# The tile of the masked scores as a fifth room, by turns, for the gates that multiply the pooled products

## The chip, the core and the metric

The kernel runs on one core of one Trainium2 chip. The core has a matrix engine (TensorE, PE in the profile, with its weight loads listed as PEld), a vector engine (VectorE, DVE), a scalar engine (ScalarE, ACT), a general engine (GpSimd, POOL), and SyncE (SP), whose queue issues nearly all DMA transfers. Each engine works through its own list of instructions in order and waits at an instruction until what it needs is there. On-chip tiles lie in SBUF; matrix products are accumulated in banks of PSUM.

The metric is the device time in microseconds (us) of one execution. Lower is better.

## The reference, cut to what matters

One decoder block on a sequence of 1024 tokens with 1024 channels, in float32. The projection of the input is split into parts for a gated recurrence (branch a), a pooling mixer (branch b) and two gates. The change touches only how branch b meets its gate:

```
proj = x @ w_in          # -> q, f, i, o_gate, pool_v, gate_a, gate_b
a = HGRN2(q, f, i) ... @ w_a
pooled[g] = causal mean over (2, 4, 8, 16)[g] tokens of pool_v[g] - pool_v[g]
b = concat_g(pooled[g] @ w_pool[g]) * pool_scale
merged = sigmoid(gate_a) * a + sigmoid(gate_b) * b
x = LN(alpha * x + merged @ w_out)
x = LN(alpha * x + relu(x @ w_up)**2 @ w_down)
```

## The kernel before, in words

Activations are kept transposed: 128 channels on the partitions, tokens along the free dimension, in two halves `u` of 512 tokens. Channels come in 8 blocks `j` of 128. Every float32 product is made of three matmuls on a high and a low part of each operand. ScalarE makes the high part (a CAST) and VectorE the low part (a subtraction). The large projections use a seven-product scheme (helper `pair`, lines 219, 221 and 222 for its matmuls), and the recurrence over 16 half-heads is woven between these products. For TensorE the order of instructions is the order of the code in this stage; for the other engines and the DMA queues the planner sets it from its own costs and the dependencies.

When the recurrence is over, the products of the pooling branch are woven in the same way between the products of the gates 6 and 7 (`pool_products`, called through `beside` with the counts of `POOL_AFTER`). There are 16 of them, and this text numbers them 1 to 16 in the order in which they run. Group `g` (0 to 3) and token half `u` give two each, one for each channel block `j = 2g + i`. So product 5 is block 2 with half 0, product 10 is block 5 with half 0; products 13 and 15 are those of block 7, which go another way (line 903) and are of no concern here. For each of the other 14:

- a room `t` of 128 x 512 is taken (line 896) and the gate `sigmoid(gate_b)`, which was put into DRAM earlier as `gbd[j][u]`, is loaded into it by SP (line 898: "load n" below);
- TensorE makes the product with six matmuls into a PSUM bank of the tag `tr`, of which there are two (lines 114 to 116, by `mm3` in line 900), so that product n + 2 needs the bank of product n;
- VectorE reads the bank, multiplies by the scale and by the gate in the room, and writes the result into the room (line 905: "multiplication n");
- SP stores the room to DRAM as `pbd[j][u]` (line 906: "store n").

In the kernel before, all these rooms come from the tag `f`, a ring of 4 that was used by the recurrence earlier (`RINGS`, `f=4`). So load n + 4 goes into the room of product n and waits until store n has landed. As SP issues in order, whatever stands behind a waiting load in its list waits too.

The tile `att` (128 x 4 x 128, that is 512 numbers on each partition) holds the masked scores of the recurrence. VectorE writes it for every half-head with a copy under the mask (line 1116), and TensorE reads it as the weights of the products with the values (line 1153). It was set to zero once, and the places outside of the mask have to stay zero as long as the recurrence runs. It is not used after the last half-head.

Of the kernel before, what the change touches and what calls it, by code (L numbers as in the profile page):

```python
# [52 lines left out]
def tile_hybrid_block(  # L53
# [36 lines left out]
    def nm(s):  # L90
        seq[0] += 1
        return f"{s}_{seq[0]}"
# [7 lines left out]
    def ps_tile(tag="pj", bufs=4):  # L100
        if tag == "hg":
            hg_tags.append(hg_tags.pop(0))
            tag, bufs = hg_tags[-1], 1
        return pp.tile([P, HALF], F32, tag=tag, name=nm("ps_" + tag), bufs=bufs)

    def f(t):
        return t.bitcast(F32)


    def mm3(ps, terms):  # L110

        n = len(terms)
        for i, (wh, wl, xh, xl) in enumerate(terms):
            PE.matmul(ps, wh, xh, start=i == 0, stop=False)  # L114
            PE.matmul(ps, wh, xl, start=False, stop=False)  # L115
            PE.matmul(ps, wl, xh, start=False, stop=i == n - 1)  # L116
# [8 lines left out]
    def split(src, tile_of):  # L125
        hi, lo = tile_of(), tile_of()
        A.copy(hi, src)
        V.tensor_sub(lo, src, f(hi))
        return hi, lo
# [130 lines left out]
    @contextmanager  # L260
    def behind_weight(n=-1):

        with tc.issue_after(hi_of[n]), tc.issue_after(lo_of[n]):
            yield
# [195 lines left out]
    def row_tile():  # L460
        return w_tile().rearrange("p k c -> p (k c)")
# [259 lines left out]
    def loaded(src, tile_of):  # L721
        t = tile_of()
        nc.sync.dma_start(out=t, in_=src)
        return t
# [31 lines left out]
    with tc.tile_pool(name="tmp", bufs=1, side="right", reuse_waits="tile") as tmp:  # L756
# [3 lines left out]
        att = hgp.tile([P, CH, P], F32, name="att")  # L760
# [11 lines left out]
        def tt(tag, dtype=F32):  # L772
            pool = tmp if tag in ("q", "f", "og", "v") else hgp
            return pool.tile([P, HALF], dtype, tag=tag, name=nm(tag), bufs=RINGS.get(tag, 1))
# [77 lines left out]
        def pool_products():  # L852

            def ring(*tags):
                tags = list(tags)
                def tile(dtype=F32):
                    tags.append(tags.pop(0))
                    return tt(tags[-1], dtype)
                return tile

            pod_tile, w_tiles = ring("tA", "tA", "st", "st", "tH", "tH"), ring("tD", "tE", "tF", "og")

            def wide(t):
                return t.rearrange("p (k c) -> p k c", c=2 * P)

            def load(g, u):
                raw = None
                if not u:
                    raw = loaded(w_pool[g].rearrange("(k p) c -> p k c", p=P), lambda: wide(tt("tC")))
                return raw, [loaded(pod[2 * g + i][u], pod_tile) for i in range(2)]  # L870

            def parts(g, u, raw, pods):
                with behind_weight():
                    if raw is not None:
                        w_parts[g] = split(raw, lambda: wide(w_tiles(F32R)))
                    made = []
                    for t in pods:
                        hi, lo = row_tile(), row_tile()
                        pool_parts[:] = A.copy(hi, t).ins, V.tensor_sub(lo, t, f(hi)).ins
                        made.append((hi, lo))  # L880
                    return made

            w_parts = {}
            todo = [(g, u) for g in range(CH) for u in range(2)]
            soon = [load(*todo[0]), load(*todo[1])]
            pl = parts(*todo[0], *soon.pop(0))
            yield
            for n, (g, u) in enumerate(todo):
                if n + 2 < len(todo):
                    soon.append(load(*todo[n + 2]))  # L890
                wh, wl = w_parts[g]
                for i in (0, 1) if g < CH - 1 else (1, 0):
                    w = slice(i * P, (i + 1) * P)
                    j = 2 * g + i
                    final = j == KT - 1
                    t = tt("v") if final else tt("f")
                    if not final:
                        nc.sync.dma_start(out=t, in_=gbd[j][u])
                    ps = ps_tile("tr", 2)
                    mm3(ps, [(wh[:, c, w], wl[:, c, w], *pl[c]) for c in range(2)])  # L900
                    if final:
                        held[u] = t
                        A.activation(t, ps, AF.Copy, scale=pscale[:, j : j + 1])
                    else:
                        V.scalar_tensor_tensor(t, ps, pscale[:, j : j + 1], t, ALU.mult, ALU.mult)
                        nc.sync.dma_start(out=pbd[j][u], in_=t)
                    if i == (1 if g < CH - 1 else 0) and soon:
                        pl = parts(*todo[n + 1], *soon.pop(0))
                    yield
# [312 lines left out]
        with tc.manual_schedule(engines={mybir.EngineType.PE}):  # L1222
            turns = turning[0] = recurrence()
            output_gates(0)
            for what, j in ORDER:
                if what == "inputs":
                    head_inputs(j)
                else:
                    dict(gates=gates, pooled=pooled, output_gates=output_gates)[what](j)
            finish_pending()  # L1230
            stream = pool_products()
            next(stream)
            for j, counts in POOL_AFTER.items():
                turning[0] = beside(stream, counts)
                gates(j)
                finish_pending()
            for _ in turns:
                pass
            turning[0] = iter(())
# [373 lines left out]
    for b in range(NBLK):  # L1613
# [3 lines left out]
        if last:  # L1617

            for ring in (dh, dw):
                t = fw.tile([P, M, 2, HALF], F32R, tag="draw", name=nm("dx"), bufs=2)  # L1620
                ring[:0] = [(t[:, n], t[:, n + 1]) for n in (0, 2)]
        for i, (name, slot, chain, fresh, (u, nh)) in enumerate(steps):
# [13 lines left out]
            for c in range(CH):  # L1636
                t = u * CH + c
# [49 lines left out]
```

## Time and profile before

| | us |
|---|---|
| median of 3 runs | 1437.62 (1436.34 to 1438.64) |
| profiled execution, its own time | 1434.66 |
| profiled execution, span from first to last instruction | 1433.0 |
| TensorE busy in that span | 1420.8 |
| VectorE, ScalarE, GpSimd busy | 1099.2, 753.2, 110.9 |
| mean granted TensorE clock | 0.999 |

The profile gives busy time by engine, then by line of the code, and for idle time what ended it. A row such as `PE ps_tr L114 <- DVE f L905: 1.4, 1, 1.4` reads: TensorE, before an instruction of line 114 that writes a tile `ps_tr`, waited for a VectorE instruction of line 905 that wrote a tile `f`, 1.4 us in total, once, longest 1.4. In a timeline each row gives start, duration, engine, line, operation, output and inputs, and in brackets the idle time just before and what ended it. Numbers of buffers are left out of the names.

### The profile page before, as it was taken

The numbers are of one execution on the slowest core, as the hardware profiler recorded it, in microseconds if no ns is written. First come the engines' busy times: TensorE is split into PE (matmuls) and PEld (weight loads), VectorE is DVE, ScalarE is ACT, GpSimd is POOL, SyncE is SP. The second block draws the span as 40 slices with busy tenths as digits, with TensorE's granted clock in tenths as the row PEclk, the third lists the DMA queues.
The fourth block names the chain that finished last, engine by engine and source line by source line (L and its number), as shares of the span: only waits on it lengthen the run. The fifth ranks groups of instructions, "written<-read, shape, count | busy, mean of one in ns | idle before, by whom it ended". The sixth has DMA issues, their size and how long they took to land.

```text
span 1433.0 us, 21208 instructions
## 1 busy us (share of the span) xinstructions
PE 1420.8 (99%) x7499; PEld 1180.1 (82%) x7499; DVE 1099.2 (77%) x1832; ACT 753.2 (53%) x1376; POOL 110.9 (8%) x300
## 2 busy tenths in 40 slices
PE   9999999999999999999999999999999999999997
PEld 7888888888888888878888888888888888888886
DVE  6967887897797796679965697666666887777978
ACT  5445566566656656455522376555556433433534
POOL 0002011111212110100003000000000100000000
PEclk9999999999999999999999999999999999999999
DMA  7142254444444546899551315444457864444422
GB/s 272 60 140 89 90 131 148 126 115 150 113 118 133 150 123 190 237 322 340 182 198 74 103 59 188 153 159 161 162 177 243 299 235 146 150 151 157 132 74 118
DMA packets 187179, 228.18 MB, mean 159 GB/s; under 512 B 12576, under 2 KB 111168, under 8 KB 187072
## 3 DMA queue, kind: packets, MB, share of 16 engines
q1 hardware_dynamic: 180464, 210.94, 44.6%
q0 software_dynamic: 5824, 13.63, 4.7%
q10 hardware_dynamic: 784, 2.25, 0.5%
q8 instruction: 59, 0.97, 0.3%
q14 instruction: 48, 0.39, 0.1%
HBM read 149.70 MB, written 77.07 MB: 158 GB/s over the span
## 4 chain that ended last, share of the span: by engine, by line
PE 95%; DVE 2%; DMA 1%; ACT 1%; issue 1%; POOL 0%; DVEq 0%; ACTq 0%; SPq 0%; POOLq 0%
PE ps_pj L219 16%; PE ps_pj L222 16%; PE ps_pj L221 16%; PE ps_pj L1565 4%; PE ps_pj L1566 4%; PE ps_pj L1564 4%; PE ps_pj L115 2%; PE ps_pj L114 2%; PE ps_pj L116 2%; PE ps_tr L1566 2%; PE ps_tr L1565 2%; PE ps_tr L1564 2%; PE ps_hg L219 1%; PE ps_sc L219 1%; PE ps_sc L222 1%; PE ps_hg L221 1%
## 5 line engine op out<-in xcount | busy, mean ns | idle before, releaser
L219 PE MATMUL ps_pj<-act,w 128*128 128x512 f32 x1068 | 419.9, 393 | 0.3 <-ACT c L303 0.2
L222 PE MATMUL ps_pj<-act,w 128*128 128x512 f32 x1068 | 415.3, 390 | 0.0
L221 PE MATMUL ps_pj<-act,w 128*128 128x512 f32 x1068 | 415.3, 389 | 0.0
L256 ACT CAST w<-raw 128x512 fp32r<-128x512 f32 x303 | 187.7, 621 | 255.4 <-PE ps_pj L221 169.7
L257 DVE TENSOR_TENSOR w<-raw,w 128x512 fp32r<-128x512 f32 x303 | 207.2, 686 | 93.6 <-ACT w L256 92.3
L219 PEld LDWEIGHTS ps_pj<-act,w 128*128 128x128 f32 x1068 | 200.5, 188 | 44.1 <-ACT c L303 1.3
L222 PEld LDWEIGHTS ps_pj<-act,w 128*128 128x128 f32 x1068 | 200.5, 188 | 42.4
L221 PEld LDWEIGHTS ps_pj<-act,w 128*128 128x128 f32 x1068 | 200.6, 188 | 40.5
L1526 ACT CAST act<-act 128x1024 fp32r<-128x1024 f32 x66 | 67.0, 1050 | 108.2 <-issue 35.0
L1527 DVE TENSOR_TENSOR act<-act,act 128x1024 fp32r<-128x1024 f32 x66 | 79.4, 1220 | 18.1 <-ACT act L1526 18.1
L1566 PE MATMUL ps_pj<-act,act 128*128 128x512 f32 x240 | 93.0, 389 | 0.0
L1565 PE MATMUL ps_pj<-act,act 128*128 128x512 f32 x240 | 93.0, 389 | 0.0
L1564 PE MATMUL ps_pj<-act,act 128*128 128x512 f32 x240 | 92.5, 389 | 0.0
L307 DVE TENSOR_TENSOR c<-c,ps_pj 128x512 f32<-128x512 f32 x91 | 62.1, 682 | 32.5 <-PE ps_pj L222 31.8
L303 ACT COPY c<-ps_pj 128x512 f32<-128x512 f32 x92 | 53.3, 581 | 3.0 <-PE ps_pj L222 1.9
L1564 PEld LDWEIGHTS ps_pj<-act,act 128*128 128x128 f32 x240 | 45.0, 188 | 9.4
L1565 PEld LDWEIGHTS ps_pj<-act,act 128*128 128x128 f32 x240 | 45.0, 188 | 9.4
L1566 PEld LDWEIGHTS ps_pj<-act,act 128*128 128x128 f32 x240 | 45.0, 188 | 9.3
L312 DVE TENSOR_TENSOR raw<-raw,raw 128x512 f32<-128x512 f32 x43 | 29.6, 689 | 25.5 <-DMA raw<-in_w_in_dram 16.1
L1435 ACT ACTIVATE c<-c 128x512 f32<-128x512 f32 x61 | 38.5, 632 | 1.7
L1434 ACT ACTIVATE c<-c 128x512 f32<-128x512 f32 x46 | 29.0, 632 | 16.4 <-DVE c L307 16.4
L751 POOL DMA_DIRECT2D s<-og x28 | 24.9, 1161 | 133.2 <-DVE og L1177 133.2
(433 smaller groups left out, 2684.6 us busy)
## 6 DMA issues: line engine op xcount, KB each, us to landing
h<-c SPq DMA_DIRECT2D x106, 256.0 KB, 3.0
raw<-in_w_in_dram SPq DMA_DIRECT2D x100, 256.0 KB, 3.3
act<-h SPq DMA_DIRECT2D x78, 256.0 KB, 3.0
draw<-in_w_down_dram SPq DMA_DIRECT2D x16, 1024.0 KB, 8.2
raw<-in_w_up_dram SPq DMA_DIRECT2D x56, 256.0 KB, 2.9
hf<-h SPq DMA_DIRECT2D x34, 256.0 KB, 3.0
s<-og POOLq DMA_DIRECT2D x28, 256.0 KB, 6.4
v<-v SPq DMA_DIRECT2D x16, 256.0 KB, 3.5
```

Source lines behind the costliest of these rows:

```text
L219: PE.matmul(ps, wh[:, k], th, start=first and k == 0, stop=False, skip_group_check=True)
L221: PE.matmul(ps, wh[:, k], tl, start=False, stop=False, skip_group_check=True)
L222: PE.matmul(ps, wl[:, k], th, start=False, stop=k == CH - 1, skip_group_check=True)
L256: hi_of.append(A.copy(hi, src).ins)
L257: lo_of.append(V.tensor_sub(lo, src, f(hi)).ins)
L303: noted(A.copy(t, ps))
L307: last_add[0] = V.tensor_add(t, t, ps).ins
L1526: A.copy(hi, src)
L1527: V.tensor_sub(lo, src, f(hi))
L1564: PE.matmul(ps, hh[:, w], wh, start=fresh and n == 0, stop=False, skip_group_check=True)
L1565: PE.matmul(ps, hh[:, w], wl, start=False, stop=False, skip_group_check=True)
L1566: PE.matmul(ps, hl[:, w], wh, start=False, stop=n == M - 1, skip_group_check=True)
```

## The change

Every fifth room is no longer taken from the ring `f`. It is the tile `att`, seen as 128 x 512. The counter `rooms_used` counts all 16 products, those of block 7 included, so `att` is the room of products 5 and 10 (product 15 is of block 7 and takes its own tile as before).

```diff
-            w_parts = {}
+            w_parts, rooms_used = {}, [0]
...
                     final = j == KT - 1
-                    t = tt("v") if final else tt("f")
+                    rooms_used[0] += 1
+                    t = tt("v") if final else tt("f") if rooms_used[0] % 5 else att.rearrange("p c q -> p (c q)")
                     if not final:
                         nc.sync.dma_start(out=t, in_=gbd[j][u])
```

The lines below it move down by one (line 898 becomes 899, 905 becomes 906, 906 becomes 907). The two kernels have the same instructions in the same order on TensorE, VectorE, ScalarE and GpSimd, but for two multiplications of line 906 that now work on `att`. Only SP's list differs, between the loads for the first pooled products and the end of the 14 loads.

The first place is SP's list just behind the recurrence. `po` is a stored pooled input and `st`, `tA`, `tH` are the tiles that it is loaded into, `raw` a block of weights, `ga` a store of a gate. The last number of a name is the number of the buffer. Before:

```order
L723 DMA st_6613<-po_1_993 128x512
L723 DMA tA_6611<-po_0_994 128x512
L723 DMA st_6615<-po_1_995 128x512
L723 DMA tH_6683<-po_0_996 128x512
L230 DMA raw_6923<-in_w_in_dram 128x4x128
```

And now:

```order
L723 DMA st_6613<-po_1_993 128x512
L899 DMA att<-gb_0_980 128x512
L723 DMA tA_6611<-po_0_994 128x512
L723 DMA st_6615<-po_1_995 128x512
L723 DMA tH_6683<-po_0_996 128x512
L230 DMA raw_6922<-in_w_in_dram 128x4x128
```

Load 5 (`gb_0_980` is `gbd[2][0]`) has moved up to here. It stood 18 rows further down, behind store 1.

The second place is SP's list in the middle of the pooled products, from store 5 on (`pb_0_1012`). Stores are named `pb`, loads of the gates are those out of `gb`: `gb_1_983` is the gate of product 8, `gb_0_984` of 9, `gb_0_986` of 10, `gb_1_985` of 11, `gb_1_987` of 12. `gb_0_988<-c` is a store of another gate. Before:

```order
L906 DMA pb_0_1012<-f_6840 128x512
L898 DMA f_6900<-gb_1_983 128x512
L723 DMA st_7011<-po_1_1005 128x512
L906 DMA pb_0_1014<-f_6851 128x512
L723 DMA st_7013<-po_1_1007 128x512
L898 DMA f_6961<-gb_0_984 128x512
L842 DMA gb_0_988<-c_6882 128x512
L230 DMA raw_7200<-in_w_a_dram 128x4x128
L906 DMA pb_1_1013<-f_6889 128x512
L898 DMA f_6972<-gb_0_986 128x512
L906 DMA pb_1_1015<-f_6900 128x512
L898 DMA f_7015<-gb_1_985 128x512
```

And now:

```order
L907 DMA pb_0_1012<-att 128x512
L899 DMA f_6960<-gb_0_984 128x512
L723 DMA st_7009<-po_1_1005 128x512
L907 DMA pb_0_1014<-f_6850 128x512
L723 DMA st_7011<-po_1_1007 128x512
L899 DMA att<-gb_0_986 128x512
L842 DMA gb_0_988<-c_6881 128x512
L230 DMA raw_7198<-in_w_a_dram 128x4x128
L907 DMA pb_1_1013<-f_6888 128x512
L899 DMA f_7013<-gb_1_985 128x512
L907 DMA pb_1_1015<-f_6899 128x512
L899 DMA f_7024<-gb_1_987 128x512
```

The stores and the loads of other things stand as they stood. In each place in which a gate was loaded, the gate of the next product is loaded now: load 9 where load 8 was, load 10, into `att`, where load 9 was, and in the same way load 8 where load 7 was, some rows ahead of this piece. Load 9 waits for store 4, as load 8 did; the second load into `att` waits for store 5, which is the store out of `att`.


## The prediction

> **What bounds the kernel now.** I read the page first, then the waits of TensorE, then the chain that ended last around the one wait that remains, and then the timelines of the engines in that stretch.
>
> ```profile
> PE 1420.8 (99%) x7499; PEld 1180.1 (82%) x7499; DVE 1099.2 (77%) x1832; ACT 753.2 (53%) x1376; POOL 110.9 (8%) x300
> ```
>
> TensorE is busy for 1420.8 of 1433.0 us. The change takes no matmul away, so all that it can win lies in TensorE's idle time. The waits of TensorE over the whole span (total, times, longest):
>
> ```profile
> PE ps_hg L480 <- POOL ident masks.py:199: 1.8, 1, 1.8
> PE ps_tr L114 <- DVE f L905: 1.4, 1, 1.4
> PE ps_tr L177 <- DVE x L204: 0.7, 1, 0.7
> PE ps_sc L538 <- DVE c L580: 0.5, 1, 0.5
> PE ps_pj L219 <- ACT c L303: 0.2, 1, 0.2
> ```
>
> One of the five is at the code that is changed: a matmul of a pooled product waited, once, for the multiplication of line 905. The chain that ended last tells what stood behind it (start, duration, what):
>
> ```profile
> 604.32 0.56 DVE f L905
> ...
> 606.29 4.09 DMA pb<-f
> 610.45 7.33 DMA f<-gb
> 617.85 0.76 DVE f L905
> 618.66 0.50 PE ps_tr L114
> ```
>
> Multiplication 4 (604.32) is stored at 606.29; the store lands 4.09 us later; load 8, which needs the same room, starts at 610.45 and takes 7.33 us; multiplication 8 starts at 617.85; and product 10, which needs the bank of product 8, starts at 618.66. So a ring of four rooms did end last here, and the longest link is a load. The stretch by ten microseconds (busy time of PE, PEld, DVE, ACT, POOL, clock, DMA share, GB/s):
>
> ```profile
> 600.00:610.00 10.00, 10.00 (x45) 8.15 (x45) 8.81 (x14) 5.10 (x9) 0.45 (x1) 1.00 0.80 259
> 610.00:620.00 10.00, 8.61 (x38) 6.71 (x37) 4.28 (x7) 4.05 (x8) 0.65 (x2) 1.00 1.02 354
> 620.00:630.00 10.00, 10.00 (x45) 8.00 (x44) 8.07 (x14) 4.84 (x10) 0.55 (x1) 1.00 0.85 278
> ...
> 650.00:660.00 10.00, 10.00 (x46) 8.28 (x45) 10.00 (x18) 8.75 (x17) 0.00 (x0) 1.00 0.93 311
> ```
>
> The load fell into the ten microseconds in which the DMA engines were full (share 1.02). On both sides of it TensorE has no gap at all, at the full clock.
>
> **What the wait cost TensorE.** Its timeline at product 10, and the starts of products 11, 12 and 13, which are used below:
>
> ```profile
> 616.64 0.39 PE L115 MATMUL ps_tr<-w,tD 128*128 128x512 f32 x1
> 616.87 0.40 PE L116 MATMUL ps_tr<-w,tE 128*128 128x512 f32 x1
> 618.66 0.50 PE L114 MATMUL ps_tr<-w,tD 128*128 128x512 f32 x1 [1.39 <-DVE f L905]
> ...
> 622.91 0.40 PE L114 MATMUL ps_tr<-w,tD 128*128 128x512 f32 x1
> ...
> 624.31 0.48 PE L114 MATMUL ps_tr<-w,tD 128*128 128x512 f32 x1
> ...
> 628.51 0.40 PE L114 MATMUL ps_tr<-w,tF 128*128 128x512 f32 x1
> ```
>
> Matmuls here start 0.23 us apart (616.64 to 616.87), so product 10 would have started at 617.10. It started at 618.66: the wait cost 1.56 us, of which the row shows 1.39 as idle. That is the largest thing the change can take away in this execution.
>
> **The change part by part.** SP's list has the old times of the places into which the loads move:
>
> ```profile
> 564.42 0.32 SPq L723 DMA_DIRECT2D st<-po  x1
> 565.81 0.32 SPq L723 DMA_DIRECT2D tA<-po  x1
> ...
> 604.45 0.32 SPq L898 DMA_DIRECT2D f<-gb  x1
> ...
> 610.45 0.32 SPq L898 DMA_DIRECT2D f<-gb  x1
> ...
> 614.53 0.32 SPq L898 DMA_DIRECT2D f<-gb  x1
> ...
> 618.96 0.32 SPq L898 DMA_DIRECT2D f<-gb  x1
> ```
>
> The times from issue to landing of the loads at 604.45 and at 614.53, each asked for by itself, are these (minimum, median and maximum of one):
>
> ```profile
> DMA to landing us min/median/max: 2.7/2.7/2.7
> DMA to landing us min/median/max: 6.3/6.3/6.3
> ```
>
> VectorE's multiplications 7 to 10, with what it did between the first two:
>
> ```profile
> 611.79 0.75 DVE L905 SCALAR_TENSOR_TENSOR f<-ps_tr,prm,f 128x512 f32<-128x512 f32 x1 [0.25 <-PE ps_tr L116]
> 612.90 0.69 DVE L257 TENSOR_TENSOR w<-raw,w 128x512 fp32r<-128x512 f32 x1 [0.36 <-ACT w L256]
> 617.85 0.75 DVE L905 SCALAR_TENSOR_TENSOR f<-ps_tr,prm,f 128x512 f32<-128x512 f32 x1 [4.26 <-DMA f<-gb]
> ...
> 620.91 0.75 DVE L905 SCALAR_TENSOR_TENSOR f<-ps_tr,prm,f 128x512 f32<-128x512 f32 x1 [0.50 <-DMA pb<-f]
> ...
> 623.49 0.75 DVE L905 SCALAR_TENSOR_TENSOR f<-ps_tr,prm,f 128x512 f32<-128x512 f32 x1 [1.24 <-PE ps_pj L222]
> ```
>
> *Load 8* takes the place at 604.45. With the landing of that place, 2.7 us, the gate is there at 607.15; with the longest one near by, 7.33, at 611.78. VectorE comes to multiplication 8 at 613.59 (612.90 + 0.69) in either case and is done at 614.34. Product 10 wants the bank at 617.10, so 1.56 us come back, at both ends of that bound.
>
> *What is late next.* Load 9 stands at 610.45, the slow place. With 7.33 us it lands at 617.78, multiplication 9 ends at about 618.6, and product 11 wants its bank at 621.35 (622.91 less 1.56): 2.7 us in hand. Load 10, into `att`, stands at 614.53; with 6.3 us it lands at 620.83, multiplication 10 ends at 621.6, and product 12 wants the bank at 622.75 (624.31 less 1.56): 1.1 us in hand, the least of all. Load 11 stands at 618.96, where the old load 10 was waited for until 623.49; multiplication 11 could end at 624.2 and product 13 wants its bank at 626.95. So none of the next three waits comes into being, with these landings. The stores that the loads wait for are the same as before in every place (store 4 at 610.45, store 5 at 614.53), so SP stands still as long as before, in the same places:
>
> ```profile
> SPq L898 <- DMA pb<-f: 18.0, 8, 3.1
> ```
>
> *Load 5, moved to just behind the recurrence.* It waits for the last read of `att`, and the load of `tA` behind it waited for the matmul after that one anyway:
>
> ```profile
> 565.12 0.39 PE L1153 MATMUL ps_hg<-v,att 128*128 128x128 f32 x2
> ...
> 588.13 0.40 PE L114 MATMUL ps_tr<-w,tD 128*128 128x512 f32 x1
> ```
>
> So `att` is free at about 565.5, the issue takes 0.32 us, and what is behind it on SP comes at most 0.4 us later. What it delays feeds product 1 at 588.13 and later, 22 us on, so I take zero on TensorE; the bounds are 0 and 0.4.
>
> *Two multiplications on `att` in place of `f`.* Same shape, the same 0.75 us; the bound is a few hundredths either way, and VectorE's idle time here (5.72 of 10 us in 610 to 620) covers it. *The memory of `att`* is now in use until store 10 has landed. It is issued behind multiplication 10, so it lands by about 630 even with 7.33 us, while other tiles of its pool are read by the last pooled product until
>
> ```profile
> 636.62 0.39 PE L116 MATMUL ps_tr<-w,og 128*128 128x512 f32 x1
> ```
>
> and later, so what is laid there afterwards should not notice. Zero, with nothing in the trace to make it a gain.
>
> The sum is 1.56 us less, on TensorE, which then runs on without a gap. The sum is made against the profiled execution, 1434.66, which would come to 1433.10. That execution is 2.96 us shorter than the median of 1437.62, and less than any of the three timed runs. Against the median the forecast is **1436.1**, or 0.11% less. A difference under 0.2%, 2.87 us, is about what a measurement of this kernel can't tell from no change.
>
> A rule weighed against this: the load of 256 KB at 610.45 took 7.33 us, and the same load at 604.45 took 2.7. The Trainium skill, "DMA: Bandwidth & Descriptors", section "Anatomy of one DMA", puts one transfer at about 2.0 us plus its bytes at 436 GB/s, an estimate of 2.6 us here. The quick load agrees with it and the slow one doesn't. By that rule load 8 would have landed in time at 610.45 already, and this change would be worth nothing.
>
> **The rivals.**
>
> *Nothing comes of it.* There are two ways. In the timed runs the load at 610.45 may land as fast as its neighbour at 604.45; then it is there at 613.15, ahead of VectorE at 613.59, and there was no wait to remove. Or TensorE, 1.56 us ahead, is held up again in 640 to 680: from 650 to 660 VectorE is busy for 10.00 of 10 us. For it: landings between 2.7 and 7.33 within six microseconds. Against it: TensorE has no gap at VectorE's fullest stretch, and VectorE loses a wait of 4.26 us as well. The time: 1437.6.
>
> *More than 0.2% faster.* The timed runs lose 2.96 us (median) that the profiled execution does not, and its other waits of TensorE sum to 3.2 us. A wait that hangs on a landing in a full stretch is one that can differ between executions. If all of the 2.96 is lost here, the change wins 4.52 us: 1433.1. The 0.2% is passed when 1.31 of the 2.96 lie here. Against it: the start and the end of the kernel depend on loads and stores too, and nothing shows where the 2.96 lie.
>
> *Slower.* The wait goes to product 12, where the least is in hand. It starts at 614.53 + landing + 0.8 (multiplication and the step to TensorE). It is later than in the kernel before if load 10 takes more than 9.0 us to land, and the kernel is slower by over 0.2% from 11.9 us on: 1440.5. For it: the DMA engines are full there. Against it: the longest such load in this stretch took 7.33 us.
>
> **How the numbers follow.** The forecast, some 1.56 us won, has a chance of 0.40, with a range of its own of 1435.3 to 1436.9; nothing won 0.24; more than 0.2% won 0.27; slower by over 0.2%, by this way or one I don't see, 0.09. The first two fall within 0.2%, so that has 0.64. The range that leaves out no more than 2 in 10 goes from just under the gain of 4.52 us, 1432.9, to 1438.6, which is 1 us above nothing won, for the scatter of the runs (1436.34 to 1438.64).
>
> **What would show it.** Right: no wait of TensorE for line 906 in the list of its waits; load 5 issued at about 565.5 and load 8 about 6 us earlier than before; product 10 starting 0.23 us behind the last matmul of product 9; VectorE's wait for a gate before multiplication 8 gone, and a short one before multiplication 9 or 10 instead; the span near 1431.4. Wrong: a wait of line 114 on the multiplication at product 11 or 12; a new idle time of TensorE between 640 and 700; or a span that differs by more than the 1.56 us that stand here to be won.

## The result, and the profile after

The changed kernel takes 1434.38 us (median of 22 runs, 1431.70 to 1438.11), the kernel before 1436.34 (22 runs, 1433.63 to 1440.21). The ratio is 0.9986, with a 95% interval of 0.998 to 0.9993: some 2 us less, between 1.0 and 2.9. That is a real gain, and a small one. The profiled execution of the changed kernel took 1432.78 us, its span is 1431.1 (before: 1434.66 and 1433.0).

The waits of TensorE in the changed kernel (total, times, longest; the change adds one line ahead of them, so what were lines 898, 905 and 906 are now 899, 906 and 907):

```profile
PE ps_hg L480 <- POOL ident masks.py:199: 1.8, 1, 1.8
PE ps_tr L177 <- DVE x L204: 0.7, 1, 0.7
PE ps_sc L538 <- DVE c L580: 0.5, 1, 0.5
PE ps_pj L219 <- DVE c L307: 0.4, 1, 0.4
PE ps_pj L219 <- ACT c L303: 0.2, 1, 0.2
```

The wait of 1.4 us for the multiplication is gone, and no wait for line 906 stands in its place. The fourth row is new; it lies at 490.94, a hundred microseconds ahead of the change, and two more executions of the kernel before have it too (0.6 us, below). SP's list of the changed kernel shows where the loads 5, 8, 9, 10 and 11 went:

```profile
565.31 0.32 SPq L899 DMA_DIRECT2D att<-gb  x1
...
604.40 0.32 SPq L899 DMA_DIRECT2D f<-gb  x1
...
610.29 0.32 SPq L899 DMA_DIRECT2D f<-gb  x1
...
614.66 0.32 SPq L899 DMA_DIRECT2D att<-gb  x1
...
618.32 0.32 SPq L899 DMA_DIRECT2D f<-gb  x1
```

VectorE's multiplications 8, 9 and 10:

```profile
613.32 0.74 DVE L906 SCALAR_TENSOR_TENSOR f<-ps_tr,prm,f 128x512 f32<-128x512 f32 x1
...
617.11 0.75 DVE L906 SCALAR_TENSOR_TENSOR f<-ps_tr,prm,f 128x512 f32<-128x512 f32 x1 [0.28 <-PE ps_tr L116]
...
620.10 0.75 DVE L906 SCALAR_TENSOR_TENSOR att<-ps_tr,prm,att 128x512 f32<-128x512 f32 x1 [1.17 <-DMA att<-gb]
```

Multiplication 8 runs at 613.32 without a wait. VectorE waits for a load at multiplication 10 now, but that costs TensorE nothing. TensorE's timeline at the last matmul of product 9 and the first ones of products 10, 12 and 13:

```profile
616.68 0.39 PE L116 MATMUL ps_tr<-w,tE 128*128 128x512 f32 x1
616.91 0.40 PE L114 MATMUL ps_tr<-w,tD 128*128 128x512 f32 x1
...
622.46 0.40 PE L114 MATMUL ps_tr<-w,tD 128*128 128x512 f32 x1
...
626.62 0.40 PE L114 MATMUL ps_tr<-w,tF 128*128 128x512 f32 x1
```

Product 10 starts 0.23 us behind the matmul ahead of it. From the start of product 1 to that of product 13 the changed kernel needs 38.68 us (587.94 to 626.62), the kernel before 40.38 (588.13 to 628.51): 1.70 us. This stretch is the measure used below, since it leaves out what happens ahead of it. Ahead of product 1 the two executions differ by 0.19, behind product 13 not at all (804.5 us to the end of the span in both).

### The profile page after: what moved, and what is told of

It is laid out like the page before. It is cut to its first block, busy times and chain, and to the rows that moved or that the text cites. A ratio compares the mean times of both kernels' runs of the same rounds, so it can differ in the third digit from the quotient of the medians.

```text
span 1431.1 us, 21209 instructions
## 1 busy us (share of the span) xinstructions
PE 1419.9 (99%) x7499; PEld 1179.9 (82%) x7499; DVE 1099.5 (77%) x1832; ACT 753.2 (53%) x1376; POOL 110.9 (8%) x300
## 4 chain that ended last, share of the span: by engine, by line
PE 95%; DVE 2%; ACT 1%; DMA 1%; issue 1%; POOL 0%; DVEq 0%; SPq 0%; ACTq 0%; POOLq 0%
PE ps_pj L219 16%; PE ps_pj L222 16%; PE ps_pj L221 16%; PE ps_pj L1566 4%; PE ps_pj L1565 4%; PE ps_pj L1567 4%; PE ps_pj L115 2%; PE ps_pj L116 2%; PE ps_pj L114 2%; PE ps_tr L1566 2%; PE ps_tr L1567 2%; PE ps_tr L1565 2%; PE ps_sc L219 1%; PE ps_hg L222 1%; PE ps_sc L222 1%; PE ps_hg L219 1%
## 5 line engine op out<-in xcount | busy, mean ns | idle before, releaser
L221 PEld LDWEIGHTS ps_pj<-act,w 128*128 128x128 f32 x1068 | 200.6, 188 | 40.6
```

Source lines behind the costliest of these rows:

```text
L221: PE.matmul(ps, wh[:, k], tl, start=False, stop=False, skip_group_check=True)
```

## The experiments

In the table, "stretch" is the time from the first matmul of product 1 to that of product 13 in TensorE's timeline of the profiled execution. The medians come from five groups of runs, each with its own runs of the kernel before.

| kernel | product 1 starts | stretch | median, and before beside it | ratio (95%) |
|---|---|---|---|---|
| before, three executions | 588.13, 588.77, 589.50 | 40.38, 40.55, 40.72 | | |
| after, three executions | 587.94, 590.43, 588.95 | 38.68, 38.68, 38.68 | 1434.38, 1436.34 | 0.9986 (0.998 to 0.9993) |
| after, timed again | | | 1434.24, 1436.08 | 0.999 (0.9981 to 0.9999) |
| first turn only | 588.73 | 38.67 | 1435.13, 1435.80 | 0.9994 (0.9985 to 1.0003) |
| second turn only | 592.09 | 42.49 | 1437.66, 1435.80 | 1.0019 (1.001 to 1.0028) |
| three rooms | 590.86 | 46.22 | 1440.01, 1435.80 | 1.0026 (1.0015 to 1.0038) |
| four rooms, three loads held | 588.63 | 41.11 | 1436.74, 1435.80 | 1.0012 (1.0003 to 1.002) |
| the same, load 8 behind store 5 | 588.13 | 40.59 | 1437.22, 1435.75 | 1.001 (1.0 to 1.0019) |
| after, loads 1 and 2 later | 588.16, 587.69 | 38.68, 38.68 | 1432.61, 1436.08; 1432.70, 1436.18 | 0.9975 (0.9965 to 0.9985); 0.9978 (0.997 to 0.9987) |
| before, loads 1 and 2 later | 587.33 | 39.39 | 1433.81, 1436.18 | 0.9978 (0.997 to 0.9987) |

**Is the wait the kernel's own?** Two more profiled executions of the kernel before, and one more of the changed kernel.

> The kernel before, unchanged, a second profiled execution. Theory (the wait at product 10 belongs to the kernel, not to that one execution): load 8 near 610.5 takes 6 to 8 us, TensorE waits 1.0 to 1.8 us for line 905 at product 10. Rival (it was that execution's): load 8 lands in under 4 us and there is no such wait. The part of the scatter that is not here should show as other waits or starts ahead of product 1 (588.13 in the first look), which the change doesn't touch.

> The kernel before, unchanged, a third profiled execution. Theory: as in the second look, a wait of 1.0 to 1.8 us at product 10, and product 13 starting 40.2 to 40.6 us behind product 1 (628.51 less 588.13 in the first look, 38.7 in the changed kernel). Rival: no wait there.

> The changed kernel, a second profiled execution. Theory: no wait of TensorE for line 906, product 10 starts 28.8 to 29.1 us behind product 1 as in the first look (616.91 less 587.94). Rival (the margins at products 11 and 12 were luck): a wait of 0.3 us or more at product 11, 12 or 13.

TensorE's timeline at product 10, in the second and the third execution of before:

```profile
619.29 0.50 PE L114 MATMUL ps_tr<-w,tD 128*128 128x512 f32 x1 [1.38 <-DVE f L905]
```

```profile
620.17 0.50 PE L114 MATMUL ps_tr<-w,tD 128*128 128x512 f32 x1 [1.54 <-DVE f L905]
```

The wait belongs to the kernel: 1.39, 1.38 and 1.54 us. Load 8 was issued at 611.30 and 611.86 there and multiplication 8 began at 618.49 and 619.37, 7.2 and 7.5 us later. The changed kernel has no wait for line 906 in any of its executions. The third stretch of before is 40.72, just over what was expected (40.6). In these two executions multiplication 10 ends at 625.05 and 625.93, and product 12 starts 1.56 and 1.60 us behind product 11 where 1.39 is its own pace: a second, small delay, since product 12 needs the bank of product 10, which the first execution just misses (1.40). What the second execution of after shows is a loss elsewhere (its waits of TensorE, the two that matter):

```profile
PE sc L1100 <- ACT q L1081: 1.6, 1, 1.6
...
PE ps_pj L219 <- DVE c L307: 0.6, 1, 0.6
```

Both lie between 484 and 494. Product 1 starts at 590.43 there, 2.5 us later than in the first execution, and the span is 1434.1. So here the time was lost ahead of the change; an experiment below finds what does it.

**Which turn of `att` does it?**

```diff
-                    t = ... tt("f") if rooms_used[0] % 5 else att...
+                    t = ... tt("f") if rooms_used[0] != 5 else att...
```

> The tile of the masked scores is the room of load 5 only; loads 9 and 10 go back to the four rooms. Theory (what counts is how early load 8 and load 10 may be issued): load 8 still stands early (near 604.4), so product 10 doesn't wait for multiplication 8. But load 10 now waits for store 7 and stands near 618.3, where load 11 stood; with a landing of 4.4 to 5 us multiplication 10 ends near 623.5, and product 12 wants its bank at 622.5: a wait of TensorE for line 906 of about 1 us at product 12, so a gain of 0.3 to 0.9 us over the kernel before, and about 1 us slower than the changed kernel. Rival (the first turn alone does it, the wait at product 10 was the only one in reach): no wait of TensorE for line 906, span within 0.2 us of the changed kernel.

The rival was right in the place of the change: no wait for line 906, and a stretch of 38.67. (The span, 1432.5, is 1.4 us above that of the changed kernel and not within 0.2: 0.8 of it lies ahead of product 1 and 0.6 behind product 13.) Load 10 does stand at 618.09, as expected (behind store 6, not store 7 as the expectation has it). But it had landed when multiplication 10 began, under 4 us later. VectorE's timeline, and then TensorE's at product 12, of this kernel:

```profile
622.04 0.75 DVE L906 SCALAR_TENSOR_TENSOR f<-ps_tr,prm,f 128x512 f32<-128x512 f32 x1 [2.33 <-PE ps_pj L222]
```

```profile
623.25 0.40 PE L114 MATMUL ps_tr<-w,tD 128*128 128x512 f32 x1
```

The first row puts the wait down to a matmul of line 222; multiplication 10 reads nothing of that matmul, and the time at which load 10 landed is not in the trace. Multiplication 10 ends at about 622.8 and product 12 begins on time at 623.25. The whole run of products stands 0.8 us later here than in the changed kernel (product 1 at 588.73), which the expectation did not count. So the second turn is not needed, with some 0.4 us in hand. The median shows a gain of 0.7 us, with an interval that takes in both no gain and that of the changed kernel; it doesn't tell them apart.

```diff
+                    t = ... tt("f") if rooms_used[0] != 10 else att...
```

> The tile of the masked scores is the room of load 10 only. Theory: loads 5 to 9 stand where they stood in the kernel before, load 8 is issued near 610.4 with the DMA engines full, so product 10 waits for multiplication 8 by 1.0 to 1.6 us; the time is that of the kernel before within 0.3 us. Rival (any fifth room in the ring gives the gain): no such wait, 1.5 to 2 us faster than before.

The wait at product 10 did stay (1.31 us), and the theory holds in that. But this kernel is 1.9 us slower than before, which neither expected. Its list of SP shows why:

```profile
587.82 0.32 SPq L842 DMA_DIRECT2D gb<-c  x1
594.81 0.32 SPq L899 DMA_DIRECT2D att<-gb  x1
595.22 0.39 SPq L230 DMA_DIRECT2D raw<-in_w_in_dram  x1
...
596.72 0.38 SPq L907 DMA_DIRECT2D pb<-f  x1
```

With `att` free since 565, load 10 was moved up to just behind the store that writes its own gate (587.82). It has to wait until that store has landed, and SP stands for 7 us. The weight load behind it comes 3.1 us after the start of product 1, where in the kernel before it came 0.6 us ahead of it (587.53). All that stands behind it on SP is late too. The next weight load of line 230 goes out at 602.57, 3.2 us later than in the kernel before when both are counted from product 1, and VectorE's line 312, which reads such blocks, stands still for 5.50 us (2.36 in the kernel before; the row names the load of `tC`, issued 0.47 us behind the block, which line 312 doesn't read):

```profile
608.19 0.69 DVE L312 TENSOR_TENSOR raw<-raw,raw 128x512 f32<-128x512 f32 x1 [5.50 <-DMA tC<-in_w_pool_dram]
```

The low part of pooled values and the multiplication behind it on VectorE are late by that, and TensorE waits for both at products 5 and 6, ahead of its wait at product 10 (two of its waits in this kernel):

```profile
PE ps_tr L114 <- DVE f L906: 1.8, 2, 1.3
...
PE ps_tr L115 <- DVE w L879: 1.2, 1, 1.2
```

A room that is free early lets the load go early, and an early load can block the queue. In the change under study load 5 has that place, and its gate had been stored long before.

**Fewer rooms.**

```diff
+            w_parts, rooms = {}, [tt("f") for _ in range(3)]
...
-                    t = tt("v") if final else tt("f")
+                    t = tt("v") if final else rooms[0]
```

(the list is turned by one at each product that is not final)

> The kernel before with three rooms in turn instead of four. Theory (the ring of rooms sets when loads start): load 8 waits for store 5 and stands near 614.5; with a landing of 6.3 us multiplication 8 ends near 621.6 and product 10, which wants its bank at 617.1, is 4.5 us late; further loads wait for the next store as well, so 5 to 9 us slower than before in all. Rival (the wait at product 10 is the DMA engines' fullness alone, whatever the rooms): within 1 us of the kernel before, with the same wait of 1.4 us.

The rooms set the starts of the loads, as the theory has it: the stretch is 5.7 us longer than the mean of before (46.22 against 40.55), and the median 4.2. The profiled execution is the slowest of this kernel's eight runs (1443.23). The place was one product off: load 7 stands at 613.33 and takes 7.1 us, so product 9 is the first to wait. The size has a part that nobody expected. TensorE's timeline of this kernel at product 9, and then five microseconds each (busy time of PE, PEld, DVE, ACT, POOL, clock, DMA share, GB/s):

```profile
621.32 0.50 PE L114 MATMUL ps_tr<-w,tD 128*128 128x512 f32 x1 [2.73 <-DVE f L906]
...
625.92 0.63 PE L114 MATMUL ps_tr<-w,tD 128*128 128x512 f32 x1
```

```profile
615.00:620.00 5.00, 3.59 (x16) 2.63 (x14) 0.00 (x0) 2.32 (x4) 0.55 (x1) 1.00 1.01 345
620.00:625.00 5.00, 3.05 (x7) 1.98 (x8) 3.89 (x6) 0.00 (x0) 0.12 (x1) 0.68 0.89 313
625.00:630.00 5.00, 5.00 (x16) 3.93 (x15) 2.57 (x5) 1.76 (x3) 0.43 (x1) 0.63 0.71 245
```

The waits for line 906 sum to 4.0 us, 2.6 more than in the kernel before. The granted clock accounts for the other 3.1 us: 0.68 and 0.63 over ten microseconds is 3.45 us, of which a part fell into the waits.

**What makes load 8 slow?** In the kernel before, the three loads of raw pooled values and weights for the next group (`tC`, `tA`, `tA`, line 723) stand just ahead of load 8. Here they are issued behind it:

```diff
-                    soon.append(load(*todo[n + 2]))
+                    with tc.issue_after(gate[0]) if n == 4 else nullcontext():
+                        soon.append(load(*todo[n + 2]))
...
-                        nc.sync.dma_start(out=t, in_=gbd[j][u])
+                        gate[0] = nc.sync.dma_start(out=t, in_=gbd[j][u]).ins
```

> The kernel before with its four rooms; only the three loads of raw gates for the next group that stood ahead of load 8 on SP are issued behind it. Theory (the 7.33 us of load 8 are the transfers issued just ahead of it: three loads and a store, about 0.74 us each at 354 GB/s): load 8, still issued near 610 behind store 4, lands in 3 to 4.5 us, product 10 doesn't wait or by less than 0.4 us, and 1.2 to 1.9 us are gained without a fifth room. Rival (the landing is slow for another reason than these three): it stays at 6.5 to 7.5 us, the wait at product 10 stays at 1.2 to 1.6 us, and the time is that of the kernel before.

Load 8, issued at 610.71, taken alone (minimum, median and maximum of one):

```profile
DMA to landing us min/median/max: 3.2/3.2/3.2
```

So most of its 7.2 to 7.5 us comes of transfers issued just ahead of it, and product 10 does not wait (617.59, 0.23 us behind product 9). Store 5 had left from ahead of load 8 too in this kernel; in the next one it is back there, and load 8 still lands in 3.6 us, so it is the three loads that make the difference. The gain did not follow. The chain that ended last in this kernel:

```profile
606.52 4.17 DMA pb<-f
...
613.25 6.44 DMA pb<-f
...
619.76 4.93 DMA f<-gb
624.71 0.76 DVE f L906
625.52 0.50 PE ps_tr L114
```

SP stood at load 8 until store 4 had landed, and store 5, now behind it, left at 611.08 instead of 609.20. Store 6 and load 10 met the transfers that had been put off, and product 12 waits for 2.20 us. The next kernel also holds load 8 behind store 5 (`stores` is the list of the stores), so that store 5 and load 9 keep their places:

```diff
+                        with tc.issue_after(stores[4]) if (n, i) == (3, 1) else nullcontext():
+                            gate[0] = nc.sync.dma_start(out=t, in_=gbd[j][u]).ins
```

> The three loads for the next group are held behind load 8 as before, and load 8 is held behind store 5, so that store 5 no longer stands behind SP's wait for store 4: loads 8 and 9 have their old places, near 610.5 and 614.5, with four rooms. Theory (the run before lost its gain because store 5 left SP 2 us late, so that load 9 started 2 us late): load 8 lands in about 3.3 us, product 10 doesn't wait; load 9 lands about 6.3 us after 614.5, so product 11 waits 0 to 0.8 us and nothing behind it; 0.8 to 1.5 us faster than the kernel before. Rival (a ring of four rooms passes any gain on to the next load): a wait of 1 to 2.2 us at product 11 or 12, the time of the kernel before within 0.7 us.

Load 8 lands in 3.6 us and product 10 begins at 617.10, on time. The chain that ended last:

```profile
612.20 6.27 DMA pb<-f
618.49 5.14 DMA f<-gb
623.65 0.76 DVE f L907
624.46 0.50 PE ps_tr L114
```

The rival was right in the wait: store 6 now takes the 6 us, load 10 follows it, and product 12 waits for 1.64 us. The stretch is 40.59, that of before. The median is 1.5 us above that of before (interval 0 to 2.7), more than the 0.7 that the rival allowed; this profiled execution lies near the fastest run and doesn't show why. In these kernels with four rooms the full stretch catches one link of the ring or the next. The fifth room leaves the links slow (load 9 took 6.1 us in the changed kernel, load 10 5.3) and gives each one more product's time.

**The scatter.** The weight load of line 230 near 473 stands behind loads 1 and 2, whose products come at 588. VectorE's line 312 waits for it, and the waits of TensorE from 484 to 494 hang on that. In the changed kernel with one more edit, loads 1 and 2 are issued behind it (`weights_loaded` is the list of these weight loads):

```diff
+                        with tc.issue_after(weights_loaded[75]) if rooms_used[0] in (1, 2) else nullcontext():
+                            nc.sync.dma_start(out=t, in_=gbd[j][u])
```

> The changed kernel with one more change, far ahead of product 1: loads 1 and 2, which SP issues near 471.3 though their products come at 588, are issued behind the weight load of line 230 that follows them near 473.2. Theory (the same collision in another place: the looks of before and after differ in what TensorE loses between 484 and 494, nothing to 2.2 us, because that weight load lands late behind the two gate loads): the weight load goes out 1 to 1.5 us earlier, VectorE's line 312 starts 1 to 2 us earlier, and the waits of lines 1100 and 219 there shrink by 0.4 to 1.2 us; product 1 starts 0.4 to 1.2 us earlier on the average, and the time is 0.4 to 1.2 us less than that of the changed kernel. Rival (GpSimd's three stores, issued from 473 to 476, fill the DMA engines whatever SP does): the waits there stay between 0.4 and 2.2 us, the time is that of the changed kernel within 0.4 us.

The weight load did not go out earlier (473.88; the store of `o` ahead of it holds it). But it landed sooner; its row, and VectorE's wait for it (line 315 here):

```profile
DMA to landing us min/median/max: 4.0/4.0/4.0
```

```profile
477.97 0.69 DVE L315 TENSOR_TENSOR raw<-raw,raw 128x512 f32<-128x512 f32 x1 [1.83 <-DMA raw<-in_w_in_dram]
```

In three executions each of before and after, the same load took 5.2, 6.1, 5.8 and 5.5, 7.8, 5.9 us. In all eleven executions with loads 1 and 2 in their old place, of whatever kernel, it took 5.2 to 8.2 us; in the other two kernels with these loads held (below) it took 4.2 and 3.7. TensorE has no wait between 484 and 494, the runs lie within 1431.89 to 1433.34, and the median is 1.6 us below that of the changed kernel in the same group of runs, a little more than expected. This is the fastest version: 0.9975 of the kernel before. The changed kernel beside it:

> The changed kernel unchanged, timed again beside the run before it on the same chip. Theory: 1.5 to 2.2 us faster than the kernel before (the stretch from product 1 to product 13 takes 38.7 us against 40.4 to 40.7 in the three looks of before), no wait of TensorE for line 906. Rival (part of the first figure was the scatter ahead of product 1): 0.8 to 1.4 us.

1.8 us less by the medians, no wait for line 906, a stretch of 38.68 again. The two kernels with and without the fifth room, both with loads 1 and 2 held:

> The kernel before, with four rooms, and loads 1 and 2 issued behind the weight load near 473. Theory (two separate collisions, whose costs add): no waits of 0.4 us or more between 484 and 494, runs within some 2 us of each other, 1.2 to 2.0 us faster than the kernel before; the wait of 1.4 to 1.6 us at product 10 stays, and product 13 starts 40.3 to 40.8 us behind product 1. Rival (the two are one: with loads 1 and 2 out of the way, load 8 lands sooner or the gain is that of the fifth room again): no wait at product 10, or no gain.

> The changed kernel with loads 1 and 2 behind the weight load, timed again beside the run before it, so that the fifth room is the only difference between two kernels that have lost the scatter near 490. Theory: 1.5 to 2.0 us less than the run before it, with little overlap of the two sets of times; 3 to 4 us faster than the kernel before. Rival (part of the fifth room's gain was the scatter): under 1.2 us less.

With four rooms 1433.81 (1432.49 to 1434.59), with five 1432.70 (1431.88 to 1434.87): 1.1 us. That is the rival's figure (under 1.2) and not that of the theory, though the two sets of times overlap: the medians of runs drawn from them at random differ by 0.3 to 1.8, so the theory's 1.5 is not ruled out. The profiled execution with four rooms shows the rival's sign too: no wait at product 10. VectorE's multiplication 8 and TensorE at products 10 and 12:

```profile
615.48 0.75 DVE L909 SCALAR_TENSOR_TENSOR f<-ps_tr,prm,f 128x512 f32<-128x512 f32 x1 [2.69 <-DMA f<-gb]
```

```profile
616.30 0.48 PE L114 MATMUL ps_tr<-w,tD 128*128 128x512 f32 x1
...
622.47 0.50 PE L114 MATMUL ps_tr<-w,tD 128*128 128x512 f32 x1 [0.41 <-DVE f L909]
```

Load 8, issued at 609.59, needs at most 5.9 us there, product 10 is just in time, and product 12 waits for 0.41. The issues around load 8 stand where they stood in the kernel before, counted from product 1, within 0.2 us, the three loads of line 723 among them, so those loads alone do not fix what load 8 takes. One execution can't tell whether load 8 is sooner because of the held loads or differs from execution to execution; that stays open. If it differs, so does what the fifth room is worth: the profiles of four rooms have from 0.71 us (39.39 less 38.68) to 2.04 (40.72 less 38.68).

## Why the prediction was right

The forecast was 1.56 us won, from 1437.62 to 1436.1; the measurement is some 2.0 us (1.0 to 2.9) by the first comparison and 1.8 (0.1 to 2.7) by the second. It is "within 0.2%", as the likeliest case had it. In plain microseconds the 1434.38 is 1.7 below the forecast 1436.1 and just below the forecast's own range (from 1435.3), because the kernel before is itself faster than the three runs that the forecast started from: 1436.34 in 22 runs, not 1437.62. The difference between the two kernels is what was forecast, and that is what came true.

*Load 8 in the place at 604.45.* It was issued at 604.40 and landed in 2.6 us (forecast 2.7), multiplication 8 ran at 613.32 (613.59 less the 0.19 by which this execution is ahead is 613.40), and product 10 starts 1.56 us earlier counted from product 1 (28.97 us against 30.53). Right, to the figure.

*The size of the sum* was a little small: the stretch is 1.70 us shorter, not 1.56. The 0.14 that the sum had left out lie behind the wait. The matmul that follows the wait takes 0.50 us in place of 0.40 and the next one starts 0.10 later; the rest is at and behind product 12. In the other two executions of before the stretch is 1.87 and 2.04 longer, since product 12 is late there as well. So 1.56 was the delay at product 10, and not the whole price of the four rooms.

*What is late next.* Load 9, in the slow place, took 6.1 us (forecast 7.33 as the bound) and multiplication 9 waited for TensorE, not for it. Load 10 took 5.3 (forecast 6.3), multiplication 10 ended at 620.85 and product 12 wanted its bank at 622.46: 1.6 us in hand, forecast 1.1, and the least of all as said. None of the waits came. (The prediction took VectorE's wait until 623.49 as one for the old load 10; the row names a matmul of line 222, and the landing of that load is not in the trace. Nothing in the sum depends on it.)

*Load 5 behind the recurrence* was issued at 565.31 and cost nothing; the load of `tA` behind it came at 565.75 (565.81 before). *The multiplications on `att`* take 0.75 us as those on `f` do. *The memory of `att`*: no new wait of TensorE appears behind product 13, and the rest of the span is equal (804.5 us).

*The rival "nothing comes of it"* needed load 8 to land in time. It took 7.2 to 7.5 us in three executions of before. In the kernel with loads 1 and 2 held it came close (at most 5.9 us, product 10 on time): the mechanism exists, and it may be why the gain there is only 1.1 us, which one execution doesn't show. No hold-up came in 640 to 680, though VectorE is busy for 10.00 of 10 us there:

```profile
650.00:660.00 10.00, 10.00 (x46) 8.29 (x45) 10.00 (x18) 8.40 (x17) 0.00 (x0) 1.00 0.94 317
```

*The rival "more than 0.2%"* asked whether the 2.96 us between the median and the profiled execution lie in this stretch. Of these, 1.28 came of having only three runs (22 runs give 1436.34). The rest is scatter that is really there, and most of it hangs, as the rival said, on a landing in a full stretch, but another one: the weight load near 473, which neither kernel changes (DMA share 1.08 and 1.11 from 476 to 480 in the first executions of after and before). With loads 1 and 2 out of its way the runs of both kernels lie closer together (12 runs with four rooms within 2.1 us, where 23 of the kernel before beside them lie within 6). The rival failed in the place; the mechanism that it named is there.

*The rival "slower"* needed load 10 to take over 9 us. It took 5.2 to 5.8 us in the five profiled executions with both turns of `att`.

The rule that the prediction weighed, of the Trainium skill, "DMA: Bandwidth & Descriptors", section "Anatomy of one DMA", gives an estimate of 2.6 us for such a load. That section of the Trainium skill fits transfers issued by GpSimd, which the prediction did not say, and the loads here are issued by SP. In the five executions with both turns of `att`, loads 7 and 8, ahead of the full stretch, are close to it all the same (2.5 to 2.7 us); loads 9 and 10, in it, are not (5.2 to 6.5). By that estimate alone the change would have been worth nothing, and the trace decided against it.

## What to carry to other kernels

Where a ring of buffers ends last in a stretch in which the DMA engines are full, moving transfers about may only pass the wait to the next link, as it did twice here; one more buffer, even a borrowed one for one turn, gave every link the time of one more step. Look through the queue ahead of every transfer that something waits for, and move behind it what is not wanted for a long time: two loads issued some 115 us before their use made most of the scatter of this kernel. (With these two held, the fifth room measured 1.1 us, where it had measured 1.8 and 2.0 by itself: two gains measured apart need not add up.) And a room that comes free early is no gain by itself, if the load into it then stands in an in-order queue waiting for the store that writes its data.

## What the runs showed of the hardware

A wait of TensorE can cost more than its length, since the granted clock may drop behind it. In the kernel with the second turn alone, TensorE idled for 1.64 us and then ran at half its rate for 3.4 us, from 488.85 to 492.24 (its timeline; matmuls 0.43 us apart instead of 0.23):

```profile
487.48 0.62 PE L1100 MATMUL sc<-q,k 128*32 128x64 f32 x16 [1.64 <-ACT q L1081]
...
488.85 0.61 PE L219 MATMUL ps_pj<-act,w 128*128 128x512 f32 x1
489.25 0.63 PE L221 MATMUL ps_pj<-act,w 128*128 128x512 f32 x1
...
492.24 0.41 PE L222 MATMUL ps_pj<-act,w 128*128 128x512 f32 x1
```

With three rooms a gap of 2.73 us, between full-size matmuls, was followed by some 6.5 us at half rate (621.94 to 628.48). But the same gap of 1.64 us at the same place in the second execution of the changed kernel, and the gap of 2.20 us with the three loads held, left the clock at 1.00:

```profile
485.00:490.00 5.00, 3.54 (x29) 2.85 (x30) 4.37 (x8) 4.98 (x17) 0.30 (x3) 1.00 0.55 171
490.00:495.00 5.00, 4.40 (x20) 3.33 (x19) 4.54 (x10) 4.04 (x10) 2.83 (x11) 1.00 0.17 51
```

The Trainium skill, "TensorE: Matmul & The Clock Gate", section "What's actually happening", tells of a window of about 3.4 us that runs freely and does not start with the kernel's own work. The half-rate stretches here (3.4 and some 6.5 us, by estimate about one and two such windows) and the fact that equal gaps do and do not lower the clock fit that; no run shows the window itself. The advice of the Trainium skill on the same page, section "Why this matters for your kernels", to have no gaps over about 3 us is no protection here: the clock fell behind gaps of 2.73 and 1.64 us. In the last 0.6 us ahead of the gap of 1.64 us TensorE ran only short matmuls of 128x32, and no run tells their part from that of the gap.
